# Moving the residuals, scalings and next transposes of the first four row blocks to later blocks in an output projection

## The chip, the cores and the metric

The kernel is one layer of a hybrid decoder, written for one core of a Trainium2 chip (trn2). The metric is device time in microseconds, the median of several runs. One execution of the kernel was also recorded by the hardware profiler; all rows quoted below come from that execution. Times in rows are microseconds from the start of its span, unless marked ns.

## The reference, cut to what matters

The input `x` has 1024 rows (tokens) of 1024 numbers, in float32.

```python
h = rmsnorm(x, mix_pre_norm)
proj = h @ w_in                               # attention and recurrence inputs
attn = rmsnorm(dilated_mixture_attention(...), attn_out_norm)
rec = hgrn2_recurrence(...)
mixed = concatenate([attn, rec], axis=-1) @ w_out          # output projection
x = x + rmsnorm(mixed, mix_post_norm)                      # residual
h = rmsnorm(x, mlp_pre_norm)                               # scaling
ff = square(relu(h @ w_ff1)) @ w_ff2
x = x + rmsnorm(ff, mlp_post_norm)
```

`rmsnorm` divides a row by the root of the mean of its squares (plus 1e-6) and multiplies by a gain. The change concerns the lines from `mixed` to the second `h`, and the transposes that prepare `h` for the product with `w_ff1`.

## The kernel before

The rows are handled in eight blocks `t` of 128 rows (`NT = 8`). Matrix products are made in three passes: each operand is split into a high part (copied by ScalarE, ACT, line 83) and a low part (the rest, subtracted by VectorE, DVE, line 84), and TensorE (PE) multiplies high by high, high by low and low by high (lines 87, 88, 89). The order of instructions on each engine is the order of the program text: nothing is reordered. Where an instruction needs a result of another engine, or a buffer that is still in use, its engine waits, and everything behind it on that engine waits too. DMAs are issued by the queue SP, also in program order.

The output projection is the loop `for t in range(NT)` at lines 1000 to 1028. Its steps, with the engines that they use:

- `late_out(t, hf)` (line 833): the matmuls of one half (512 columns) of block `t` into a PSUM bank `pwo`. The banks have the tag "mm" for even `t` and "s" for odd `t`, two banks of each; so block `t` takes the banks of block `t - 2`. For `t < NE = 4` the recurrent half of the product was made earlier and lies in SBUF as `esum`; only 4 of the 8 slices of 128 are left, that is 12 matmuls per half. From block 4 on a half has 24.
- `row_turn(t + 1, which)` (line 800): four transposes on PE (`pmt`, line 812), then the split into `mt` on ACT and DVE. It prepares the left operand of the next block. Blocks before 4 need one such call here, later ones two.
- `row_attn(t + 2)` (line 794): two DVE instructions that scale a row block (lines 796, 798). `row_norm(t + 3)` (line 777): its squares on ACT (`dm`, lines 783 and 784) and its scale on GpSimd (POOL). `row_rec(t + 3)` (line 770): a product on POOL. `row_load(t + 4)` (line 762): its DMA.
- `mixed_half(t, hf)` (line 847): for `t < 4` DVE adds the bank to `esum` (line 856), which frees the bank; then ACT squares and sums the half (`dp`, line 858). After the second half POOL makes the scale `prp` (lines 863, 79, 80). In the first half it also issues the reload of `x` for the next block (`x_again`, line 843), into a buffer `xres` of the tag "P", which has three.
- `residual(t)` (line 866): per half DVE multiplies by `prp` and the gain (line 876; for `t >= 4` it reads the PSUM bank and so frees it) and adds `x` (line 877); ACT squares and sums the result (`dx`, line 878). Then SP stores the block (`x2d`, line 879) and POOL makes the next scale `x2r`.
- `residual_b(t)` (line 883): one DVE instruction over the whole block, with `x2r` and the gain of the next norm (line 889). For `t < 4` it writes into `esum`, for `t = 4` in place, later into a slab `x2n`.
- `next_turn(t)` (line 891): for each of two halves `kh` four transposes on PE into a bank `ph` of the tag "t" (two banks, line 899), and a copy by ACT into `hraw` (line 905). `split_tokens` in iterations 4 and 6 splits two finished blocks of `hraw` into `h2` (ACT and DVE).

In iteration `t` the kernel before runs `residual(t - 1)` ahead of `mixed_half(t, 0)`, and, behind the second half's matmuls, `next_turn(t - 2)` and `residual_b(t - 1)`. After the loop follow the first matmuls with `w_ff1`, with `residual`, `residual_b` and `next_turn` of the last blocks between them.

Small columns (one number per row) come from a tag with four buffers, `c1`, by the helper `col`.

Of the kernel before, what the change touches and what calls it, by code (L numbers as in the profile page):

```python
# [8 lines left out]
F32 = mybir.dt.float32  # L9
# [8 lines left out]
P = 128  # L18
# [3 lines left out]
NT = T // P  # L22
# [13 lines left out]
def hymba_layer(ctx, tc, x, w_in, w_out, w_ff1, w_ff2, g_pre, lb_logits, g_mix, g_post,  # L36
# [9 lines left out]
    tp = ctx.enter_context(tc.tile_pool(name="tiny", bufs=4))  # L46
# [3 lines left out]
    def slab(tag, name, dtype=F32, shape=(P, T)):  # L50
        return sp.tile(list(shape), dtype, tag=tag, name=name,
                       bufs={"S": 9, "T": 9, "P": 3, "BT": 2, "V8": 2, "R": 1}[tag])

    def bank(tag, name):
        return ps.tile([P, 512], F32, tag=tag, name=name,
                       bufs={"mm": 2, "s": 2, "t": 2, "pv": 2}[tag])

    def half(name, dtype=F32):
        return sp.tile([P, 512], dtype, tag="half", name=name, bufs=2)

    def col(name, n=1):
        return tp.tile([P, n], F32, tag=f"c{n}", name=name)
# [14 lines left out]
    def rsqrt_mean(dst, ssum, n, width):  # L77
        t = col("ms", width)
        G.tensor_scalar(t, ssum, 1.0 / n, EPS, op0=ALU.mult, op1=ALU.add)  # L79
        G.tensor_tensor(out=dst, in0=t, in1=nhalf[:, :width], op=ALU.pow)  # L80
# [653 lines left out]
    rows, xress, mts, pmo, gains, scales = {}, {}, {}, {}, {}, {}  # L734
    AL = (AH // 2 - 1) * P

    def load_gain(name, tag, src):
        gains[name] = slab(tag, name)
        nc.sync.dma_start(out=gains[name], in_=src.partition_broadcast(P))
# [19 lines left out]
    def early_sum(t):  # L759
        return early["sum"][t // 2][:, t % 2]  # L760

    def row_load(t):
        row = rows[t] = slab("S", f"row{t}")
        c = AW if t < NE else 0
        nc.sync.dma_start(out=row[:, c:AW + AL], in_=mix_dram[t * P:(t + 1) * P, c:AW + AL])
# [11 lines left out]
    def row_norm(t):  # L777
        row = rows[t]
        dump = half(f"dm{t}")
        ss = col("ass", 2)  # L780
        sa = col("asa")
        ra = scales["row", t] = tp.tile([P, 1], F32, tag="era", name=f"era{t}") if t < NE else col("ara")
        S.activation(dump[:, :AL], row[:, AW:AW + AL], AF.Square, accum_out=ss[:, 0:1])
        S.activation(dump[:, AL:AW], row_fin(t), AF.Square, accum_out=ss[:, 1:2])
        G.tensor_tensor(out=sa, in0=ss[:, 0:1], in1=ss[:, 1:2], op=ALU.add)
        rsqrt_mean(ra, sa, AW, 1)

    def row_gain(t):

        row, gmix = rows[t], gains["gmix"]  # L790
        G.tensor_tensor(out=row[:, AW:AW + AL], in0=row[:, AW:AW + AL], in1=gmix[:, AW:AW + AL], op=ALU.mult)
        G.tensor_tensor(out=row[:, AW + AL:], in0=row_fin(t), in1=gmix[:, AW + AL:], op=ALU.mult)

    def row_attn(t):
        row, gmix, ra = rows[t], gains["gmix"], scales.pop(("row", t))
        V.scalar_tensor_tensor(row[:, AW:AW + AL], row[:, AW:AW + AL], ra, gmix[:, AW:AW + AL],
                               op0=ALU.mult, op1=ALU.mult)
        V.scalar_tensor_tensor(row[:, AW + AL:], row_fin(t), ra, gmix[:, AW + AL:], op0=ALU.mult, op1=ALU.mult)

    def row_turn(t, which, late=False):  # L800

        if t < NE and which == 0:
            dst = early["mt"][t // 2][:, t % 2]
        else:
            if (t, 1) not in mts and (t, 0) not in mts or t < NE:
                mts[t] = slab("V8", f"mt{t}", F32R, (P, 2, 2, 4, P))
            dst = mts[t][:, which]
        mts[t, which] = dst
        src = rec_row(t) if which == 0 else rows[t][:, AW:]
        pt = bank("pv" if late else "t", f"pmt{t}_{which}")  # L810
        for j in range(4):
            TE.transpose(pt[:, j * P:(j + 1) * P], src[:, j * P:(j + 1) * P], ident)
        split_into(dst[:, 0], dst[:, 1], pt.rearrange("p (j c) -> p j c", j=4))
# [19 lines left out]
    def late_out(t, hf):  # L833
        pm = pmo[t, hf] = bank("s" if t % 2 else "mm", f"pwo{t}_{hf}")
        if t >= NE:
            run(out_mm(t, hf, 0, pm, True, False))
        run(out_mm(t, hf, 1, pm, t < NE, True))
# [5 lines left out]
    def x_again(t):  # L843
        xress[t] = slab("P", f"xres{t}")
        nc.sync.dma_start(out=xress[t], in_=x[t * P:(t + 1) * P, :])

    def mixed_half(t, hf):

        if hf == 0:
            if t + 1 < NT:  # L850
                x_again(t + 1)
            scales["mix", t] = col("pss", 2)
        src = pmo[t, hf]
        if t < NE:
            whole = early_sum(t)[:, hf * 512:hf * 512 + 512]
            V.scalar_tensor_tensor(whole, src, scales["row", t], whole, op0=ALU.mult, op1=ALU.add)
            src = pmo[t, hf] = whole
        S.activation(half(f"dp{t}{hf}"), src, AF.Square, accum_out=scales["mix", t][:, hf:hf + 1])
        if hf == 1:
            s2 = scales.pop(("mix", t))  # L860
            s1 = col("ps1")
            rp = scales["mix", t] = col("prp")
            G.tensor_tensor(out=s1, in0=s2[:, 0:1], in1=s2[:, 1:2], op=ALU.add)
            rsqrt_mean(rp, s1, D, 1)

    def residual(t):
        xr = xress[t]
        rp = scales.pop(("mix", t))
        s4 = col("x2h", 2)
        s3 = col("x2s")  # L870
        r3 = scales["x2", t] = col("x2r")
        for hf in range(2):
            sl = slice(hf * 512, hf * 512 + 512)
            src = pmo.pop((t, hf))
            add = src if t < NE else half(f"ad{t}{hf}")
            V.scalar_tensor_tensor(add, src, rp, gains["gpost"][:, sl], op0=ALU.mult, op1=ALU.mult)
            V.tensor_tensor(out=xr[:, sl], in0=add, in1=xr[:, sl], op=ALU.add)
            S.activation(half(f"dx{t}{hf}"), xr[:, sl], AF.Square, accum_out=s4[:, hf:hf + 1])
        nc.sync.dma_start(out=x2_dram[t], in_=xr)
        G.tensor_tensor(out=s3, in0=s4[:, 0:1], in1=s4[:, 1:2], op=ALU.add)  # L880
        rsqrt_mean(r3, s3, D, 1)

    def residual_b(t):
        xr = xress[t]
        if t < NE:
            xress[t] = early_sum(t)
        elif t >= NT - 3:
            xress[t] = slab("S", f"x2n{t}")
        V.scalar_tensor_tensor(xress[t], xr, scales.pop(("x2", t)), gains["gmlp"], op0=ALU.mult, op1=ALU.mult)

    def next_turn(t):

        xr = xress.pop(t)
        th, c = t // 4, (t % 4) * P
        for kh in range(2):
            pt = bank("t", f"ph2{t}_{kh}")
            for j in range(4):
                k = kh * 4 + j
                TE.transpose(pt[:, j * P:(j + 1) * P], xr[:, k * P:(k + 1) * P], ident)
            src = pt.rearrange("p (j c) -> p j c", j=4)  # L900
            if t % 4 == 0:
                hraw[kh, th] = wide.tile([P, 4, 512], F32, tag="A", name=f"hraw{kh}{th}")
                if th == 0:
                    h2[kh] = tuple(wide.tile([P, 4, 512], F32R, tag="A", name=f"h2{q}{kh}") for q in "hl")
            S.activation(hraw[kh, th][:, :, c:c + P], src, AF.Copy)
# [91 lines left out]
    load_gain("gpost", "T", g_post)  # L997
    load_gain("gmlp", "T", g_mlp)
    h2, hraw = {}, {}
    for t in range(NT):  # L1000
        late_out(t, 0)
        if t > 0 and t + 1 < NT:
            for which in range(t + 1 < NE, 2):
                row_turn(t + 1, which, True)
            if t + 4 < NT:
                row_load(t + 4)
        if NE <= t + 2 < NT:
            row_attn(t + 2)
        if t > 0:
            residual(t - 1)  # L1010
        mixed_half(t, 0)
        late_out(t, 1)
        if t > 1:
            next_turn(t - 2)
        if t > 0:
            residual_b(t - 1)
        if t + 3 < NT:
            row_norm(t + 3)
            if t + 3 < NE:
                row_gain(t + 3)  # L1020
        if t in (4, 6):
            for kh in range(2):
                split_tokens(kh, (t - 4) * P)
        if t == 4:
            w_get(W10, 0)
        mixed_half(t, 1)
        if NE <= t + 3 < NT:
            row_rec(t + 3)

# [584 lines left out]
    x2r, plain, praw = {}, {}, {}  # L1614
# [105 lines left out]
    t, pieces, rf = late  # L1720
# [71 lines left out]
```

## Time and profile before

| | us |
|---|---|
| median of 3 runs | 1289.68 |
| lowest and highest run | 1286.98, 1290.79 |
| profiled execution | 1289.73 |
| its span | 1287.9 |

Over the span PE is busy for 97%, DVE for 69%, ACT for 41% and POOL for 23%. The loop of the output projection runs from about 571 to 652 us.

A row of the timeline gives the start, the duration, the engine, the line, the operation with its output and inputs, the shape and the count; in brackets stands how long the engine was idle before it, and which engine, tile and line ended that. Matmuls overlap: a matmul of 512 columns lasts about 0.39 us, but the next starts after 0.23. So work on PE is measured here from start to start. A row of the windows gives the stretch, its length, the busy time of PE, PE's weight loads, DVE, ACT and POOL (with counts), the granted clock of PE as a share of full speed, the busy share of the DMA engines, and GB/s.

### The profile page before, as it was taken

The numbers are of one execution on the slowest core, as the hardware profiler recorded it, in microseconds if no ns is written. First come the engines' busy times: TensorE is split into PE (matmuls) and PEld (weight loads), VectorE is DVE, ScalarE is ACT, GpSimd is POOL, SyncE is SP. The second block draws the span as 40 slices with busy tenths as digits, with TensorE's granted clock in tenths as the row PEclk, the third lists the DMA queues.
The fourth block names the chain that finished last, engine by engine and source line by source line (L and its number), as shares of the span: only waits on it lengthen the run. The fifth ranks groups of instructions, "written<-read, shape, count | busy, mean of one in ns | idle before, by whom it ended". The sixth has DMA issues, their size and how long they took to land. (4 is left out here: it accounts for less than half of the span.)

```text
span 1287.9 us, 17288 instructions
## 1 busy us (share of the span) xinstructions
PE 1247.8 (97%) x6524; PEld 1061.3 (82%) x6524; DVE 885.1 (69%) x1524; ACT 533.3 (41%) x967; POOL 297.8 (23%) x308
## 2 busy tenths in 40 slices
PE   8999999999999998999999899999999999999997
PEld 8898989888888887887877788888878888888886
DVE  5686868675666666667658766666676776688956
ACT  6623232213555556564555322222235533344412
POOL 0000000012122223043250487575541000000012
PEclk9999999999999999898999999999999999999999
DMA  5201111123222323335242344443369454434423
GB/s 205 67 17 50 34 50 33 34 82 88 61 83 66 83 66 110 98 114 179 94 152 90 139 173 177 148 180 131 139 245 353 161 196 131 160 102 131 155 76 129
DMA packets 58578, 153.98 MB, mean 120 GB/s; under 512 B 4992, under 2 KB 12928, under 8 KB 58240
## 3 DMA queue, kind: packets, MB, share of 16 engines
q1 hardware_dynamic: 58496, 152.89, 35.1%
q8 instruction: 51, 0.84, 0.3%
q14 instruction: 31, 0.25, 0.1%
HBM read 106.73 MB, written 39.85 MB: 114 GB/s over the span
## 5 line engine op out<-in xcount | busy, mean ns | idle before, releaser
L87 PE MATMUL f<-bh,ah 128*128 128x512 f32 x392 | 152.5, 389 | 0.0
L88 PE MATMUL f<-bl,ah 128*128 128x512 f32 x392 | 152.5, 389 | 0.0
L89 PE MATMUL f<-bh,al 128*128 128x512 f32 x392 | 152.5, 389 | 0.0
L84 DVE TENSOR_TENSOR al<-ar,ah 128x1024 fp32r<-128x1024 f32 x49 | 60.6, 1236 | 48.2 <-ACT ah L83 17.6
L87 PEld LDWEIGHTS f<-bh,ah 128*128 128x128 f32 x392 | 73.6, 188 | 15.4
L89 PEld LDWEIGHTS f<-bh,al 128*128 128x128 f32 x392 | 73.6, 188 | 15.3
L88 PEld LDWEIGHTS f<-bl,ah 128*128 128x128 f32 x392 | 73.6, 188 | 15.1
L83 ACT ACTIVATE ah<-ar 128x1024 fp32r<-128x1024 f32 x49 | 52.0, 1062 | 48.8 <-DMA ar<-actd 22.0
L1707 POOL TENSOR_SCALAR fp<-fss 128x1 f32<-128x1 f32 x8 | 3.5, 432 | 267.4 <-ACT fd L1704 267.4
L670 DVE CUSTOM_DVE_ANT_0 p<-ps,bt 128x512 f32<-128x512 f32 (+2 forms) x84 | 44.3, 552 | 25.0 <-PE ps L668 24.8
L697 ACT ACTIVATE pth<-pt 128x512 fp32r<-128x512 f32 (+2 forms) x96 | 43.3, 486 | 42.3 <-PE pt L694 40.6
L698 DVE TENSOR_TENSOR ptl<-pt,pth 128x512 fp32r<-128x512 f32 (+2 forms) x96 | 50.2, 551 | 15.3 <-ACT pth L697 15.2
L681 ACT ACTIVATE p<-p,nm 128x128 f32<-128x128 f32 (+3 forms) x64 | 49.5, 773 | 9.3 <-DVE nm L676 6.2
L727 POOL TENSOR_TENSOR anat<-anat,rd 128x128 f32<-128x128 f32 x32 | 14.6, 455 | 150.5 <-DVE anat L726 146.9
L79 POOL TENSOR_SCALAR ms<-hss 128x8 f32<-128x8 f32 x4 | 0.8, 197 | 206.3 <-DVE hss L538 206.3
L83 ACT ACTIVATE bh<-br 128x1024 fp32r<-128x1024 f32 x28 | 29.7, 1060 | 43.2 <-PE f L89 37.9
L694 PE MATMUL pt<-ident,p 128*128 128x128 f32 x288 | 42.9, 276 | 4.7 <-DVE ptl L698 4.7
L1221 POOL TENSOR_TENSOR e<-x,e 128x512 f32<-128x512 f32 x14 | 20.6, 1473 | 102.5 <-DVE x L1172 102.5
L84 DVE TENSOR_TENSOR wl<-raw,wh 128x1024 fp32r<-128x1024 f32 x23 | 31.4, 1365 | 18.3 <-ACT wh L83 18.0
L694 PEld LDWEIGHTS pt<-ident,p 128*128 128x128 f32 x288 | 33.5, 141 | 9.3 <-DVE ptl L698 6.8
L711 PE MATMUL pov<-pth,v 128*128 128x256 f32 (+1 forms) x160 | 40.6, 288 | 0.0
L1574 DVE TENSOR_TENSOR acc<-f,acc 128x512 f32<-128x512 f32 x52 | 33.8, 684 | 8.3 <-PE f L89 8.3
(1615 smaller groups left out, 3905.9 us busy)
## 6 DMA issues: line engine op xcount, KB each, us to landing
ar<-actd SPq DMA_DIRECT2D x49, 512.0 KB, 3.7
raw<-in_w_in_dram SPq DMA_DIRECT2D x28, 512.0 KB, 3.6
w1r<-in_w_ff_dram SPq DMA_DIRECT2D x14, 1024.0 KB, 6.6
br<-in_w_ff_dram SPq DMA_DIRECT2D x14, 1024.0 KB, 7.2
actd<-e SPq DMA_DIRECT2D x17, 768.0 KB, 4.1
actd<-e SPq DMA_DIRECT2D x11, 1024.0 KB, 4.0
xr<-in_x_dram SPq DMA_DIRECT2D x8, 512.0 KB, 9.5
raw<-in_w_out_dram SPq DMA_DIRECT2D x8, 512.0 KB, 3.6
```

Source lines behind the costliest of these rows:

```text
L83: S.activation(hi, src, AF.Copy)
L84: eng.tensor_tensor(out=lo, in0=src, in1=f32(hi), op=ALU.subtract)
L87: TE.matmul(dst, lhs[0], rhs[0], start=start, stop=False)
L88: TE.matmul(dst, lhs[0], rhs[1], start=False, stop=False)
L89: TE.matmul(dst, lhs[1], rhs[0], start=False, stop=stop)
L670: V.tensor_tensor_reduce(out=pe[:, k0:k0 + n], in0=pS[:, :n], in1=bts[hd][:, o:o + n], scale=1.0, scalar=-3.0e38, op0=ALU.add, op1=ALU.max ...
L681: S.activation(pe[:, :nk], pe[:, :nk], AF.Exp, bias=nm[:, b:b + 1], accum_out=dn[:, b:b + 1])
L694: TE.transpose(pt[:, j * P:(j + 1) * P], pe[:, jj * P:(jj + 1) * P], ident)
L697: S.activation(hi, src, AF.Copy)
L698: V.tensor_tensor(out=lo, in0=src, in1=f32(hi), op=ALU.subtract)
L711: TE.matmul(po[:, c0:256], vst, pt[j // 4][q][:, j % 4, c0:], start=j == 0 and q == 0, stop=j == nj - 1 and q == 1)
L1574: V.tensor_tensor(out=acc_at(p, i), in0=pm, in1=acc_at(p, i), op=ALU.add)
```

## The change

Residuals, scalings and next transposes of blocks are issued at other places of the loop, given by three tables: `RES` (residual, ahead of `mixed_half(t, 0)`), `RES_B` (residual_b, ahead of RES), `TURN` (next_turn, behind the second half's matmuls). Residual 0 and 1 stand at the end of iterations 1 and 2. The places, before and after:

| block | residual, before | after | residual_b, before | after | next_turn, before | after |
|---|---|---|---|---|---|---|
| 0 | 1 | end of 1 | 1 | 2 | 2 | 3 |
| 1 | 2 | end of 2 | 2 | 3 | 3 | 4 |
| 2 | 3 | 4 | 3 | 5 | 4 | 5 |
| 3 | 4 | 5 | 4 | 6 | 5 | 6 |
| 4 | 5 | 5 | 5 | 6 | 6 | 6 |
| 5 | 6 | 6 | 6 | 7 | 7 | 7 |
| 6 | 7 | 7 | 7 | 7 | after the loop | after the loop |

Block 7 follows after the loop in both. The reload of `x` for block `r + 3` now follows residual_b of block `r`, whose buffer it takes. Two of the small columns, `prp` and `x2r`, get tags of their own with two buffers each.

```diff
     def mixed_half(t, hf):
         if hf == 0:
-            if t + 1 < NT:
-                x_again(t + 1)
             scales["mix", t] = col("pss", 2)
...
-            rp = scales["mix", t] = col("prp")
+            rp = scales["mix", t] = tp.tile([P, 1], F32, tag="prp", name=f"prp{t}", bufs=2)
...
     def residual(t):
-        r3 = scales["x2", t] = col("x2r")
+        r3 = scales["x2", t] = tp.tile([P, 1], F32, tag="x2r", name=f"x2r{t}", bufs=2)
...
+    RES = {4: (2,), 5: (3, 4), 6: (5,), 7: (6,)}
+    RES_B = {2: (0,), 3: (1,), 5: (2,), 6: (3, 4), 7: (5,)}
+    TURN = {3: (0,), 4: (1,), 5: (2,), 6: (3, 4), 7: (5,)}
     for t in range(NT):
         late_out(t, 0)
...
         if NE <= t + 2 < NT:
             row_attn(t + 2)
-        if t > 0:
-            residual(t - 1)
+        for r in RES_B.get(t, ()):
+            residual_b(r)
+        if t < 2:
+            x_again(t + 1)
+        for r in RES.get(t, ()):
+            residual(r)
         mixed_half(t, 0)
         late_out(t, 1)
-        if t > 1:
-            next_turn(t - 2)
-        if t > 0:
+        for r in TURN.get(t, ()):
+            next_turn(r)
+        for r in RES_B.get(t, ()):
+            if r + 3 < NT:
+                x_again(r + 3)
+        if t == NT - 1:
             residual_b(t - 1)
         if t + 3 < NT:
             row_norm(t + 3)
...
         mixed_half(t, 1)
+        if t in (1, 2):
+            residual(t - 1)
         if NE <= t + 3 < NT:
             row_rec(t + 3)
```

## The prediction

> **What bounds the kernel now.** I read the page first, then the granted clock by windows around the changed stage (571 to 652 us), then the timeline of each engine there. On the page TensorE (PE) is busy nearly all the time, and one slice of the changed stage shows a lowered clock.
>
> ```profile
> span 1287.9 us, 17288 instructions
> PE 1247.8 (97%) x6524; PEld 1061.3 (82%) x6524; DVE 885.1 (69%) x1524; ACT 533.3 (41%) x967; POOL 297.8 (23%) x308
> PEclk9999999999999999898999999999999999999999
> ```
>
> ```profile
> 596.00:598.00 2.00, 0.44 (x2) 0.02 (x1) 1.07 (x1) 2.00 (x8) 0.74 (x2) 1.00 1.00 295
> 602.00:604.00 2.00, 2.00 (x6) 1.51 (x6) 1.97 (x4) 0.00 (x0) 0.11 (x1) 0.50 0.00 0
> ```
>
> The second fence shows windows (length, then PE busy; the granted clock is the third number from the end). PE nearly stands still in one, and some microseconds later it is busy throughout at half clock. The timeline of PE names the place.
>
> ```profile
> 576.76 0.39 PE L87 MATMUL pwo<-woh,mt 128*128 128x512 f32 x1
> 579.49 0.60 PE L812 MATMUL pmt<-ident,row 128*128 128x128 f32 x4
> 582.47 0.39 PE L89 MATMUL pwo<-woh,mt 128*128 128x512 f32 x1
> 588.64 1.03 PE L899 MATMUL ph<-ident,esum 128*128 128x128 f32 x8
> 589.54 0.50 PE L87 MATMUL pwo<-woh,mt 128*128 128x512 f32 x1
> 592.67 1.03 PE L812 MATMUL pmt<-ident,row 128*128 128x128 f32 x8
> 596.05 0.39 PE L89 MATMUL pwo<-woh,mt 128*128 128x512 f32 x1
> 598.36 1.06 PE L899 MATMUL ph<-ident,esum 128*128 128x128 f32 x8 [1.92 <-DVE esum L889]
> 600.22 0.79 PE L87 MATMUL pwo<-wh,mt 128*128 128x512 f32 x1 [0.80 <-ACT mt L83]
> 608.63 1.03 PE L812 MATMUL pmt<-ident,row 128*128 128x128 f32 x8
> 615.76 0.48 PE L87 MATMUL pwo<-wh,mt 128*128 128x512 f32 x1
> 621.30 1.03 PE L812 MATMUL pmt<-ident,row 128*128 128x128 f32 x8
> 628.42 0.48 PE L87 MATMUL pwo<-wh,mt 128*128 128x512 f32 x1
> ```
>
> A half block of twelve matmuls takes 2.73 us (576.76 to 579.49); of 24 matmuls, 5.54 (615.76 to 621.30). At 598.36 the transposes of block 1 wait 1.92 us for its scaling (L889), and at 600.22 block 4 waits 0.80 for its split on ACT. The 24 matmuls that follow take 8.41 us (600.22 to 608.63), 2.87 too many, at half clock. Block 3's first half takes 3.13 instead of 2.73 (589.54 to 592.67), 0.40 too many. So the stage loses 1.92 + 0.80 + 2.87 + 0.40 = 6.0 us, and this is all that the change can win. The reason: blocks 0 to 3 have only half of PE's work left (twelve matmuls per half), but all of DVE's and ACT's.
>
> **What the change moves.** No instruction goes or comes; residual and residual_b of blocks 0 to 3 and next_turn of blocks 0 to 4 shift between iterations. Every engine keeps to program order, so I lay the new order along the rows. First the durations that I need.
>
> ```profile
> 580.75 0.69 DVE L84 TENSOR_TENSOR mt<-pmt,mt 128x512 fp32r<-128x512 f32 x1 [3.04 <-ACT mt L83]
> 588.91 0.58 ACT L83 ACTIVATE mt<-pmt 128x512 fp32r<-128x512 f32 x1
> 590.13 1.73 DVE L796 SCALAR_TENSOR_TENSOR row<-row,ara,gmix 128x384 f32<-128x384 f32 x1
> 592.04 0.74 DVE L876 SCALAR_TENSOR_TENSOR esum<-esum,prp,gpost 128x512 f32<-128x512 f32 x1
> 594.81 0.74 DVE L856 SCALAR_TENSOR_TENSOR esum<-pwo,era,esum 128x512 f32<-128x512 f32 x1
> 594.99 0.63 ACT L878 ACTIVATE dx<-xres 128x512 f32<-128x512 f32 x1 [0.59 <-DVE xres L877]
> 595.52 0.19 ACT L878 ACTIVATION_READ_ACCUMULATOR dx<-xres 128x1 f32 x1
> 596.93 1.28 DVE L889 SCALAR_TENSOR_TENSOR esum<-xres,x2r,gmlp 128x1024 f32<-128x1024 f32 x1 [1.37 <-POOL x2r L80]
> 598.13 0.74 DVE L856 SCALAR_TENSOR_TENSOR esum<-pwo,era,esum 128x512 f32<-128x512 f32 x1
> 610.88 1.29 DVE L84 TENSOR_TENSOR mt<-pmt,mt 128x512 fp32r<-128x512 f32 x2 [1.34 <-ACT mt L83]
> 626.72 0.74 DVE L876 SCALAR_TENSOR_TENSOR ad<-pwo,prp,gpost 128x512 f32<-128x512 f32 x1
> ```
>
> Residual costs DVE 2.77 us (592.04 to 594.81), residual_b 1.20 (596.93 to 598.13), row_attn 1.91 (590.13 to 592.04), an addition of mixed_half 0.7; the squares of a residual cost ACT 0.72 (594.99 to the end of the readout, 595.71).
>
> *First place, block 4's first matmul.* Residual(0) now stands behind block 1's second addition: pwo ends at 582.86, the addition takes DVE to 583.6, residual(0) to 586.4. ACT's squares end at 587.2, block 3's split on ACT (0.58) at 587.8 and on DVE at 588.4, just before PE wants it (588.64); the 0.40 goes. DVE then does row_attn(4) to 590.3, residual_b(0) to 591.5, two additions to 592.9, residual(1) to 595.6. ACT squares it until 596.4 and only then splits block 4, at 597.0. PE comes there, without next_turn(0) at 588.64, by 2.73 + 0.8 + 2.8 + 0.9 at 595.85. It waits 1.15, and its third matmul some 0.25 more for the low part. The old wait of 1.92 is gone, because next_turn(0) comes long after residual_b(0); what is late next is the split of block 4, behind the squares of block 1. New loss: 1.4.
>
> *Second place, block 6's first matmul.* It writes the PSUM bank of block 4, which residual(4) frees with its first L876. From the split of block 5 on DVE (610.88) to that instruction (626.72) were 15.84 us; the new iteration 5 puts residual_b(2) and residual(3) in front of it, 1.20 + 2.77, which makes 19.81. That the old residual_b(3) no longer stands on this path wins nothing, since the next item (the split of h2) waited for ACT anyway. PE's own way from block 5's transposes (608.63) to block 6 (628.42) is 19.79 and stays. So the wait is DVE's lag behind the transposes at block 5, plus 0.75 for the instruction and 0.05. The lag was 2.25 (608.63 to 610.88); the smallest in this stage was 1.26 (579.49 to 580.75). I take 2.25, because copies and squares still stand ahead of this split on ACT. The loss is 3.05, at least 2.05. Some 0.4 of it shows at next_turn(2), which waits for residual_b(2).
>
> *Third place, next_turn(4).* Iteration 6 issues next_turn(3) and next_turn(4) back to back; each takes two PSUM banks of the tag "t", which has two. So block 4's transposes wait until ACT has copied block 3's first bank.
>
> ```profile
> 639.51 0.63 ACT L878 ACTIVATE dx<-xres 128x512 f32<-128x512 f32 x1 [0.71 <-DVE xres L877]
> 640.14 0.58 ACT L858 ACTIVATE dp<-pwo 128x512 f32<-128x512 f32 x1
> 640.30 1.03 PE L899 MATMUL ph<-ident,xres 128*128 128x128 f32 x8
> 640.93 1.09 ACT L905 ACTIVATE hraw<-ph 128x512 f32<-128x512 f32 x2
> 641.09 0.48 PE L87 MATMUL pwo<-wh,mt 128*128 128x512 f32 x1
> 641.40 0.33 SPq L845 DMA_DIRECT2D xres<-in_x_dram  x1
> ```
>
> ```profile
> DMA to landing us min/median/max: 2.8/3.8/9.6
> ```
>
> Before, ACT was ready for this copy just when PE had transposed. Now residual_b(3) and residual_b(4) stand between block 7's split and residual(5) on DVE, 2 x 1.20, and all of dx, dp, hraw comes 2.40 later: dx 641.91, dp 642.55, copy 643.2 to 643.75. PE is ready at 641.1, on this clock, and goes on at 643.85: 2.75 lost. DVE can't start earlier, since block 7's split, which needs PE, stands ahead. The second next_turn itself (0.8) costs nothing new, it only comes later.
>
> *DMAs.* The reloads of x move on SP: x(6) now stands behind the store of block 5, at about 642, and lands at 646 by the median of 3.8; residual(6) uses it in the next iteration, some 8 us after the issue. The worst landing, 9.6, would cost DVE 2 us that PE doesn't wait for. x(7) still waits for next_turn(4) to free its buffer (641.40). The row loads keep their lead. The two small columns with buffers of their own add no instruction. All this is hidden.
>
> **Sum.** Old losses 6.0, new ones 1.4 + 3.05 + 2.75 = 7.2: 1.2 us longer before any clock effect. Now the clock. Besides the old stall, three waits of PE elsewhere bear on it or on what follows the stage:
>
> ```profile
> 333.64 0.50 PE L667 MATMUL ps<-kh,q 128*128 128x512 f32 x1 [1.18 <-DVE mx L670]
> 656.63 0.51 PE L1155 MATMUL f11a<-h2h,wl 128*128 128x512 f32 x1 [0.34 <-DVE wl L84]
> 715.88 0.80 PE L1155 MATMUL f12d<-T10h,ws 128*128 128x512 f32 x1 [2.55 <-DVE ws L84]
> 719.21 0.40 PE L1154 MATMUL f12d<-T11l,ws 128*128 128x512 f32 x1
> ```
>
> After the wait of 2.55, eight matmuls take 3.33 us instead of 1.85: 1.5 lost. After the old gap (596.44 to 600.22, 3.8 without a matmul, transposes inside) 2.87 was lost. The gap at block 6 has the same form (0.4 of wait, transposes, 2.6 of wait: 3.8); I take 2.2, between the two. The third has 2.75 unbroken: 1.5 by its nearest row. The first, 1.15, is left at nothing, by the wait of 1.18 at 333.64, behind which the first matmul took 0.50 and not 0.80 as at 715.88; its bound above is 1.5.
>
> [...]
>
> The profiled execution took 1289.73 (span 1287.9 and 1.8 around it), 0.05 above the median of the runs. After the stage PE and the splits hang on its last matmuls (PE's next wait is 0.34, at 656.63, for a split), so a shift goes through; the wait of 2.55 above is the most that could take some of it in, and it hangs on DVE's chain, which shifts too. Forecast: 1289.7 + 1.2 + 2.2 + 1.5 = **1294.6**.
>
> **Rivals.**
> *The clock stays up.* The two new waits come, but no half clock, or only one short stretch. For it: the wait of 1.18 cost no clock, and the new ones are each shorter than the old gap. Against it: 2.55 at 715.88. Time: 1290.9, with one stretch 1292.4; within 0.3%. [...]
> *Faster.* DVE, relieved in iterations 1 to 3, is ahead by iteration 5, and residual(4) frees its bank before PE asks. It decides at 2.25 + 0.8 = 3.05 us: DVE must reach block 5's split that much earlier against the transposes. Then the second gap and its clock go; if ACT also leads by 2.75 at next_turn(4), only the 1.4 is left: 1289.7 - 6.0 + 1.4 = 1285.1. Against it: the lag can't fall below 1.26, as the split follows the transposes.
> *The old stall does not go,* because the squares of residual(1) on ACT hold block 4's split by more than 1.15 and the clock falls there too: about 1.5 on top, 1296 to 1298.
>
> **Chances.** Forecast 0.50; clock stays up 0.37; faster 0.09; old stall too 0.04. A difference under 0.3% (3.9 us) counts as none; the forecast, +4.9, is just beyond. So slower 0.54, same 0.37, faster 0.09. Range: below, both waits with the smaller lag and no slow stretch, 1289.7 + 1.2 - 1.0 = 1289.9, less 2 for the spread of the runs; above, both stretches at 2.87 and 1.0 more at the first place, 1297.6. That is 1288 to 1298.
>
> **What would show it.** Right: no wait for L889 at next_turn(1); about 1.2 of wait for ACT's mt at block 4; PE waiting 2 to 3 us for DVE's L876 (ad) at block 6's first L87 and for ACT's hraw at the transposes of block 4; a granted clock of 0.5 for 3 to 6 us behind one or both. Wrong: no wait on L876 or hraw, or a full clock behind them.

## The result and the profile after

| | before | after |
|---|---|---|
| median of 8 runs, us | 1290.51 | 1294.39 |
| lowest and highest, us | 1286.98, 1291.62 | 1291.97, 1296.11 |
| profiled execution, us | 1289.73 | 1294.30 |
| its span, us | 1287.9 | 1292.5 |

The ratio is 1.0038, with a 95% interval of 1.0028 to 1.0048: slower by 0.38%, some 5 us. (The ratio isn't worked out from the medians; these are 3.9 us apart.)

The first view lists whom PE waited for in the kernel after, in the stretch 565 to 660 us (engine, tile and line; who was waited for; us in total, times, longest).

```profile
PE ph L897 <- ACT hraw L903: 2.4, 1, 2.4
PE pwo L87 <- DVE ad L874: 2.3, 1, 2.3
PE ph L897 <- DVE esum L887: 1.5, 1, 1.5
PE pwo L87 <- ACT mt L83: 0.9, 1, 0.9
```

The old wait of 1.92 for L889 at next_turn(1) is gone. The wait at block 4 for its split on ACT, 0.80 before, is still there with 0.88, and three others are new. All four lie in the three places of the prediction. (Behind the diff, L874, L887, L897 and L903 are the old L876, L889, L899 and L905.) The timeline of PE and, for the instructions that it waits for, of DVE and ACT, after:

```profile
570.43 0.60 PE L812 MATMUL pmt<-ident,row 128*128 128x128 f32 x4
594.55 1.03 PE L897 MATMUL ph<-ident,esum 128*128 128x128 f32 x8
596.47 0.50 PE L87 MATMUL pwo<-wh,mt 128*128 128x512 f32 x1 [0.88 <-ACT mt L83]
602.32 1.03 PE L812 MATMUL pmt<-ident,row 128*128 128x128 f32 x8
622.99 1.06 PE L897 MATMUL ph<-ident,esum 128*128 128x128 f32 x8 [1.52 <-DVE esum L887]
626.34 0.78 PE L87 MATMUL pwo<-wh,mt 128*128 128x512 f32 x1 [2.28 <-DVE ad L874]
633.52 1.03 PE L812 MATMUL pmt<-ident,row 128*128 128x128 f32 x8
639.86 1.03 PE L897 MATMUL ph<-ident,esum 128*128 128x128 f32 x8
643.29 1.86 PE L897 MATMUL ph<-ident,xres 128*128 128x128 f32 x8 [2.40 <-ACT hraw L903]
644.81 0.78 PE L87 MATMUL pwo<-wh,mt 128*128 128x512 f32 x1
656.78 1.03 PE L897 MATMUL ph<-ident,x2n 128*128 128x128 f32 x8
```

```profile
605.20 1.29 DVE L84 TENSOR_TENSOR mt<-pmt,mt 128x512 fp32r<-128x512 f32 x2 [3.07 <-ACT mt L83]
625.54 0.74 DVE L874 SCALAR_TENSOR_TENSOR ad<-pwo,prp,gpost 128x512 f32<-128x512 f32 x1
635.99 1.28 DVE L887 SCALAR_TENSOR_TENSOR esum<-xres,x2r,gmlp 128x1024 f32<-128x1024 f32 x1
637.19 1.28 DVE L887 SCALAR_TENSOR_TENSOR xres<-xres,x2r,gmlp 128x1024 f32<-128x1024 f32 x1
642.65 1.07 ACT L903 ACTIVATE hraw<-ph 128x512 f32<-128x512 f32 x2
```

The granted clock of PE, third number from the end, in windows behind the second and the third place, after:

```profile
626.00:628.00 2.00, 1.67 (x4) 1.39 (x5) 1.90 (x4) 1.16 (x4) 1.29 (x3) 0.60 0.64 262
628.00:630.00 2.00, 2.00 (x6) 1.57 (x6) 0.52 (x1) 1.39 (x5) 0.42 (x3) 0.55 0.33 135
642.00:644.00 2.00, 0.71 (x4) 0.71 (x5) 0.00 (x0) 1.73 (x6) 0.93 (x3) 0.86 0.95 299
644.00:646.00 2.00, 2.00 (x9) 1.81 (x8) 0.00 (x0) 1.41 (x3) 0.00 (x0) 0.50 0.64 234
646.00:648.00 2.00, 2.00 (x9) 1.60 (x8) 1.24 (x2) 2.00 (x3) 0.00 (x0) 0.78 0.82 240
```

A measure of the stage alone is the way from the transposes of block 1 (570.43) to those of next_turn(5) (656.78): 86.35 us. In the kernel before it was 652.07 - 570.70 = 81.37. So the stage itself is 5.0 us longer, the span of these two executions 4.6: the loss arises here. This length is used for each experiment below, because single executions also differ elsewhere (see the end).

### The profile page after: what moved, and what is told of

It is laid out like the page before. It is cut to its first block, busy times and chain, and to the rows that moved or that the text cites. A ratio compares the mean times of both kernels' runs of the same rounds, so it can differ in the third digit from the quotient of the medians.

```text
span 1292.5 us, 17284 instructions
## 1 busy us (share of the span) xinstructions
PE 1248.4 (97%) x6524; PEld 1062.3 (82%) x6524; DVE 885.7 (69%) x1524; ACT 533.1 (41%) x967; POOL 300.0 (23%) x308
```

## The experiments

The theory under test: engines keep to program order, so the place of a step in DVE's and ACT's queue makes the waits, and the two larger waits lower PE's clock, which costs extra. An instance of that order in the kernel after: DVE is idle for 6.27 us ahead of block 7's split (634.79), and the two scalings behind it in the text start only at 635.99 and 637.19; in the first run below, where they stand ahead of that split, they start at 626.72 and 629.93. The rivals stand in the expectations. The first four ran against the kernel before at a median of 1289.52, the last two at 1289.46. Gains against the changed kernel are worked out from the ratios to the kernel before, with 0.1% as 1.29 us. Ratio and medians differ by up to 0.09%, some 1.2 us, so the stage stands beside them; it comes from one execution of each kernel.

| kernel | ratio to before, 95% interval | median, us | stage, us |
|---|---|---|---|
| changed | 1.0038 (1.0028 to 1.0048) | 1294.39 | 86.35 |
| scalings first | 1.0018 (1.0007 to 1.0030) | 1292.09 | 82.46 |
| residuals swapped | 1.0021 (1.0011 to 1.0031) | 1292.69 | 84.80 |
| changed, PE's waits filled | 1.0005 (0.9996 to 1.0013) | 1291.27 | 83.22 |
| both orders, residual_b(2) early | 0.9989 (0.9979 to 0.9999) | 1289.31 | 80.97 |
| steps in DVE's gaps | 0.9968 (0.9956 to 0.9979) | 1285.40 | 76.57 |
| before, PE's waits filled | 1.0001 (0.9992 to 1.0010) | 1289.13 | 80.55 |

**Scalings first (third place alone).**

```diff
         late_out(t, 0)
+        for r in RES_B[6] if t == 6 else ():
+            residual_b(r)
         if t > 0 and t + 1 < NT:
             for which in range(t + 1 < NE, 2):
...
-        for r in RES_B.get(t, ()):
+        for r in RES_B.get(t, ()) if t != 6 else ():
             residual_b(r)
```

> Changed kernel, but in iteration 6 residual_b(3) and residual_b(4) stand ahead of block 7's split (row_turn(7)) instead of behind it. In-order theory: DVE does them in the 6.3 us that it waits for that split, dx, dp and the copy of block 3 come 2.4 us earlier, and the wait of 2.40 at the transposes of block 4 goes, and with it the half clock behind it (1.7): 1294.4 - 2.2 - 1.7 = 1290.5. The waits at block 6 (1.52 and 2.28) stay. Rival (the third wait is that of two banks too few, whatever ACT does): the wait stays at 2 us or more, 1294.

The timeline of PE at the second and the third place, and of DVE ahead of the third:

```profile
624.61 0.79 PE L87 MATMUL pwo<-wh,mt 128*128 128x512 f32 x1 [2.29 <-DVE ad L874]
639.16 1.15 PE L897 MATMUL ph<-ident,xres 128*128 128x128 f32 x8 [0.25 <-ACT hraw L903]
...
629.93 1.28 DVE L887 SCALAR_TENSOR_TENSOR xres<-xres,x2r,gmlp 128x1024 f32<-128x1024 f32 x1 [1.94 <-DMA x2d<-xres]
```

The wait of 2.40 is down to 0.25 with the same two banks, so the wait hung on the order on DVE, and through it on when ACT came to the copy, as the theory has it; the rival falls. The stage is 3.9 us shorter, as expected. The median gains less, 2.6 us by the ratios, but its interval reaches up to the expected 3.9; whether something else takes a little back, the runs don't tell. Something new shows: residual_b(4) works in place, and DVE waits 1.94 us for the store of that buffer.

**Residuals swapped (second place alone).**

```diff
-    RES = {4: (2,), 5: (3, 4), 6: (5,), 7: (6,)}
+    RES = {4: (2,), 5: (4, 3), 6: (5,), 7: (6,)}
```

> Changed kernel, but iteration 5 issues residual(4) ahead of residual(3). In-order theory: the bank that block 6 wants is freed 2.8 us earlier, the wait of 2.28 for DVE at block 6 goes to 0 to 0.3, the half clock behind it (1.6) goes, the wait of 1.5 for residual_b(2) stays: 1294.4 - 2.2 - 1.6 = 1290.6. The third place keeps 2.4. Rival (DVE has too much work in this stretch, whatever its order): the wait moves to another instruction, 1293 to 1295.

```profile
621.23 1.06 PE L897 MATMUL ph<-ident,esum 128*128 128x128 f32 x8 [1.52 <-DVE esum L887]
638.73 1.97 PE L897 MATMUL ph<-ident,xres 128*128 128x128 f32 x8 [3.73 <-ACT hraw L903]
640.35 0.78 PE L87 MATMUL pwo<-wh,mt 128*128 128x512 f32 x1
```

```profile
627.64 1.03 PE L812 MATMUL pmt<-ident,row 128*128 128x128 f32 x8
629.58 1.11 ACT L83 ACTIVATE mt<-pmt 128x512 fp32r<-128x512 f32 x2
```

The wait at block 6's first matmul is gone, as the order says. But the third wait grew from 2.40 to 3.73, so 1.3 of the 2.3 came back, with a longer half clock (6.8 us instead of 3.4). The second fence gives the reason: block 7's transposes start at 627.64, but on ACT the squares of residual(3) and all that queues behind them come first, and the split starts at 629.58, 1.9 us later (0.6 in the changed kernel, 633.52 to 634.16). So the theory was right about the second place, and the rival was right that part of the wait moves: the two places aren't independent. The stage is 1.6 us shorter, not 3.8.

**PE's waits filled (the clock alone).**

```diff
+    def fill_pe(n, tag, mt):
+        pm = bank("pv", f"fill{tag}")
+        wh = parts[WO0 + 1][0]
+        for _ in range(n):
+            TE.matmul(pm, mt[:, 0, 0], wh[:, :512], start=True, stop=True)
...
+        if t == 6:
+            fill_pe(8, "b", mts[6, 0])
         late_out(t, 0)
...
         for r in TURN.get(t, ()):
+            if r == 2:
+                fill_pe(5, "a", mts[6, 0])
+            if r == 4:
+                fill_pe(9, "c", mts[6, 0])
             next_turn(r)
```

> Changed kernel, all orders and waits kept, but PE does matmuls of no use (into a bank nobody reads) in its waits: 5 ahead of next_turn(2), 8 ahead of block 6, 9 between next_turn(3) and next_turn(4); by 0.23 each they fit into the waits of 1.52, 2.28 and 2.40. Clock theory: the waits end at the same instants, but the clock stays at 1.0 behind them, and what the half clock cost (1.6 and 1.7) is won: 1291.1. Rival (the slow matmuls there are slow for another reason, such as data just written): half clock or slow rows remain, 1294 or, with the filling in the way, more.

The matmuls go into a bank that nobody reads. Timeline of PE, and the clock by windows:

```profile
621.14 1.09 PE L897 MATMUL ph<-ident,esum 128*128 128x128 f32 x8 [0.31 <-DVE esum L887]
621.99 2.11 PE L1002 MATMUL fillb<-woh,mt 128*128 128x512 f32 x8
624.58 0.50 PE L87 MATMUL pwo<-wh,mt 128*128 128x512 f32 x1 [0.48 <-DVE ad L874]
630.16 1.03 PE L812 MATMUL pmt<-ident,row 128*128 128x128 f32 x8
```

```profile
626.00:628.00 2.00, 2.00 (x10) 1.64 (x10) 0.72 (x2) 1.29 (x6) 0.47 (x3) 1.00 0.21 88
640.00:642.00 2.00, 2.00 (x13) 1.75 (x14) 0.00 (x0) 1.74 (x4) 0.00 (x1) 1.00 0.91 287
```

Block 6 starts when DVE lets it, 55.9 us behind the start of the stage as in the changed kernel, but now at full clock: its 24 matmuls take 5.58 us (624.58 to 630.16) instead of 7.18. The stage is 3.1 us shorter (expected 3.3), the ratio falls by 0.33%. PE did 22 matmuls more and the kernel became faster, so the rival is out. Without the price of the clock the changed kernel would be nearly level with the one before. That isn't like against like, though, since the kernel before has a slow stretch of its own: with the waits filled in both (see the last run), the stage is still 2.7 us longer with the change (83.22 against 80.55).

**Both orders, and residual_b(2) early.** The edits of the first two, and `residual_b(2)` with the reload behind it in iteration 4, ahead of the split of h2.

> Both orders of the first two runs, and residual_b(2) moved into iteration 4 ahead of the split of h2, where DVE waits 4.1 us for ACT. In-order theory: all three waits behind block 5 go (1.52, 2.28, 2.40) with both half clocks (1.6, 1.7); only the wait of 0.9 at block 4 is left: 1294.4 - 9.3 = 1285.1, some 5 us faster than before. Rival (DVE and ACT bound the stage, so that waits only move): no better than 1290.

The waits at block 6 are gone, but 2.51 of the third stays:

```profile
628.80 1.28 DVE L887 SCALAR_TENSOR_TENSOR esum<-xres,x2r,gmlp 128x1024 f32<-128x1024 f32 x1 [2.04 <-POOL x2r L80]
631.20 1.28 DVE L84 TENSOR_TENSOR mt<-pmt,mt 128x512 fp32r<-128x512 f32 x2
637.31 1.46 PE L897 MATMUL ph<-ident,xres 128*128 128x128 f32 x8 [2.51 <-ACT hraw L903]
```

Residual(3), now the later of the two, delivers its scale late; residual_b(3) waits 2.04 for it and holds block 7's split on DVE, which stands behind it (631.20). ACT comes late to its part of that split too, at 629.58, as in the run with the residuals swapped; what each of the two costs was not separated. The expected 1285 was missed by 4 us: the stage is 5.4 us shorter, not 9.3. By the ratio the kernel is just faster than the one before; the medians are 0.2 us apart.

**Steps in DVE's gaps.** Blocks 0 and 1 as changed; the rest where DVE was seen waiting.

```diff
-    RES = {4: (2,), 5: (3, 4), 6: (5,), 7: (6,)}
-    RES_B = {2: (0,), 3: (1,), 5: (2,), 6: (3, 4), 7: (5,)}
-    TURN = {3: (0,), 4: (1,), 5: (2,), 6: (3, 4), 7: (5,)}
+    RES = {4: (), 5: (4,), 6: (5,), 7: (6,)}
+    RES_B = {2: (0,), 3: (1,), 4: (2,), 7: (5,)}
+    TURN = {3: (0,), 4: (1,), 5: (2,), 6: (4,), 7: (5,)}
...
         late_out(t, 0)
+        if t == 6:
+            next_turn(3)
+            residual_b(4)
...
         for r in RES.get(t, ()):
             residual(r)
+        if t == 5:
+            residual_b(3)
         mixed_half(t, 0)
...
+        if t in (5, 6):
+            x_again(t + 1)
...
+        if t == 4:
+            residual(3)
         if t in (4, 6):
...
         mixed_half(t, 1)
-        if t in (1, 2):
+        if t in (1, 2, 3):
             residual(t - 1)
```

> Changed kernel for blocks 0 and 1; from block 2 on the steps are laid where DVE sat waiting: residual(2) at the end of iteration 3, residual_b(2) early and residual(3) late in iteration 4 (ahead of the split of h2), residual_b(3) behind residual(4) in iteration 5, next_turn(3) right behind the first half of block 6 and residual_b(4) ahead of block 7's split; next_turn(4) alone at its old place. In-order theory: residual(4) is the first residual of iteration 5 and frees its bank in time (wait at block 6 0 to 0.5), the copies of block 3 are made half a block before next_turn(4) needs the banks (wait 0 to 0.3); only the 0.9 at block 4 is left, no half clock in the stage: 1294.4 - 9 = 1285, 4.5 us faster than the kernel before. Rival (DVE and ACT bound the stage, waits only move): 1288 or more.

The reloads of x for blocks 6 and 7 are issued in iterations 5 and 6. PE's wait in the stage, and the second and the third place on its timeline:

```profile
PE pwo L87 <- ACT mt L83: 0.9, 1, 0.9
```

```profile
621.74 1.03 PE L897 MATMUL ph<-ident,esum 128*128 128x128 f32 x8
628.44 1.03 PE L897 MATMUL ph<-ident,esum 128*128 128x128 f32 x8
635.65 1.03 PE L897 MATMUL ph<-ident,xres 128*128 128x128 f32 x8
```

Only the wait at block 4 is left, no transposes wait, the clock stays at 1.00, and the stage is 9.8 us shorter than in the changed kernel and 4.8 shorter than before. The median of 1285.40 beats both kernels, by 0.32% the one before (interval 0.21% to 0.44%). The rival is out: DVE and ACT had enough time, the order was what was missing. No run moved the wait at block 4.

**Before, PE's waits filled.**

```diff
+        if t == 4:
+            fill_pe(3, "b", mts[3, 1])
         late_out(t, 0)
...
+        if t == 3:
+            fill_pe(7, "a", mts[3, 1])
         if t > 1:
             next_turn(t - 2)
```

The helper `fill_pe` is that of the other filling, but its bank is one of the tag "mm".

> Kernel before, its order kept, but PE fills its two waits with matmuls of no use: 7 ahead of next_turn(1), 3 ahead of block 4 (0.23 each, into waits of 1.92 and 0.80). Both theories: the clock stays at 1.0 behind 600 us, where 2.87 was lost. Theory A (DVE's backlog was hidden behind the slow clock): with PE 2.9 us earlier, residual(4) is late for block 6, a wait of 1.4 to 2.6 for DVE's L876 appears there, and little is won, 1288.5 to 1290. Theory B (the prediction's old losses of 6.0 were all there was to win): no new wait, 1289.5 - 2.9 = 1286.6.

```profile
597.71 1.06 PE L899 MATMUL ph<-ident,esum 128*128 128x128 f32 x8 [0.34 <-DVE esum L889]
605.42 1.04 PE L812 MATMUL pmt<-ident,row 128*128 128x128 f32 x8
626.07 0.74 DVE L876 SCALAR_TENSOR_TENSOR ad<-pwo,prp,gpost 128x512 f32<-128x512 f32 x1
626.95 0.47 PE L87 MATMUL pwo<-wh,mt 128*128 128x512 f32 x1 [1.49 <-DVE ad L876]
```

The slow matmuls behind 600 us are gone, but a wait of 1.49 for residual(4) appears at block 6, where the kernel before had none. DVE reaches that instruction 56.0 us behind the start of the stage in both kernels (626.07 - 570.08 here, 626.72 - 570.70 before): it gained nothing from a faster PE. The stage is 0.8 us shorter, not 2.9, and the time is unchanged. So theory A holds: the half clock of the kernel before had hidden that DVE comes too late for block 6.

## Why the prediction was right

The forecast was 1294.6; the measured median is 1294.39. The mechanism came as forecast: three places, the named engines waited for, and a half clock behind the two larger waits. That the number is hit to 0.2 us is partly luck. The forecast started from 1289.7, the median of the kernel before in 3 runs; over 8 runs it is 1290.51, 0.8 higher. And the terms missed in both directions.

The terms are compared here from start to start, as the prediction took its own. The number in brackets on a row is smaller than what the wait costs: it counts from the end of the last matmul, and without the wait the next one would have started some 0.2 us before that end (640.30 and 1.03 long, but the next starts at 641.09). Without a wait, transposes take 0.79 to the next matmul and 24 matmuls 5.54.

- *First place.* Forecast 1.15 of wait for block 4's split behind the squares of residual(1), and 0.25 for its low part, 1.4 in all. Measured 1.44: 7.77 (594.55 to 602.32) instead of 6.33, with the same releaser. No clock was lost there, as taken (1.00 from 594 to 602), so the rival of the old stall is out. That the squares are the cause is read off ACT's rows (the split starts at 595.84, right behind them); no run tested it.
- *Second place.* Forecast 3.05 in two parts, 0.4 at next_turn(2) and the rest at block 6 for L876. Measured 4.23 (602.32 to 626.34 is 24.02, instead of 19.79), in brackets 1.52 at next_turn(2) and 2.28 at block 6. The terms account for it: DVE's lag at block 5 was 2.88 (602.32 to 605.20), not the 2.25 taken, and its way to residual(4) 20.34 (605.20 to 625.54), not 19.81. The prediction had looked only for a smaller lag, down to 1.26; it grew, and the rival *Faster*, which needs a smaller one, is out.
- *Third place.* Forecast 2.75 for ACT's copy. Measured 2.64 (639.86 to 643.29 is 3.43, instead of 0.79), in brackets 2.40. The two scalings stand ahead of residual(5) as forecast, at 635.99 and 637.19. That they are the cause is shown by moving just them: 0.25 in brackets.
- *The clock.* Forecast 2.2 and 1.5. Measured 1.64 behind block 6 (7.18 instead of 5.54), and 1.72 at the third place: the transposes of block 4 start 1.52 us ahead of the next matmul instead of 0.79, and the 48 matmuls of block 7 take 11.97 (644.81 to 656.78) instead of 10.98 (641.09 to 652.07 before). Filling the waits won 3.1 of the stage: shown. The rival "the clock stays up" is out.
- *The sum.* The new losses are 1.44 + 4.23 + 2.64 of waiting and 3.36 of clock, 11.7; forecast 10.9. The old ones, measured in the same way, are 2.08 and 1.07 of waiting, 2.87 of clock and 0.4 around block 3, 6.4; the prediction had read the two waits off the brackets and came to 6.0. That makes 5.2 more, where 4.9 was forecast. The stage grew by 5.0; the rest of 0.2 lies at its start, which was that much slower in the kernel before (8.79 from 570.70 to 579.49, against 8.62 from 570.43 to 579.05). So the second place was 1.2 too small, and the clock 0.3 and the old losses 0.4 made part of that up.
- *The bound.* That 6.0 us "is all that the change can win" stands as a bound, if 6.4 is put for it: the best order here won 4.8 of the stage. But its terms can't be won one by one. Taking away the half clock alone won 0.8 of 2.87, because the next wait, at block 6, comes out.
- *DMAs.* The reload of x for block 6 was issued at 641.80, against 642 forecast, and PE waited for none in the stage.

No single wait in the stage of the kernel after was over 2.64, and the clock fell behind two places. From the last matmul ahead of the waits to the first behind them, with transposes in between, 4.9 us passed at the second place and 4.8 us at the third. The clock also fell behind the wait of 2.54 shown at the end, which has no transposes in it. How long a gap must be for the clock to fall is not shown by these runs.

## What to carry to other kernels

Where every engine runs in program order, as in the rows here, a step that is moved away from one wait stands in front of something else (the two scalings ahead of residual(5): 2.40 us of wait at next_turn(4)): lay the new order along the durations of the old rows, engine by engine, and look for the next thing in the queue, the PSUM bank that a late reader holds and the buffer count of a tag. Put moved steps where their engine was seen waiting, not where the text has room; that turned a loss of 0.38% into a gain of 0.32% here, with as many instructions on each engine. Where a half clock followed a wait of PE, it cost a further 1.64 and 1.72 us in the stage after and 2.87 before, and matmuls of no use put into the wait are a cheap test for that price (with them the clock stayed at 1.00 from 586 to 660 in both kernels). Before a stall is counted as a gain, look for the wait that it hides.

## What the runs showed of the hardware

Up to PE's last matmul, the slow stretches have only two lengths, 3.4 and 6.8 us: in the whole profiles of the kernels before and after, and in the windows at 510 to 530, 586 to 660 and 706 to 728 us of the six others. In the kernel before, the clock was low from 599.44 to 606.28 (worked out from the windows that hold its ends, clock 0.86 at 598 to 600 and 0.93 at 606 to 608, with 0.50 in the whole windows between): 6.8 us. In the kernel after it was low from 626.4 to 629.8 and from 643.44 to 646.88: 3.4 us each, and the two start 17.04 us apart, five times 3.41. Two more start in the same profile, at 517.16 and at 721.96: 109.24 us ahead of 626.4 and 78.52 behind 643.44, which is 32 and 23 times 3.41.

Waits of one length did not cost the same in each profile. The wait of 2.55 in the next stage, which the prediction priced, shows it. First the kernel after, then the kernel before with PE's waits filled:

```profile
720.54 0.50 PE L1165 MATMUL f12d<-T10h,ws 128*128 128x512 f32 x1 [2.54 <-DVE ws L84]
```

```profile
714.42 0.50 PE L1166 MATMUL f12d<-T10h,ws 128*128 128x512 f32 x1 [2.55 <-DVE ws L84]
```

In the kernel after, the first matmul behind it still ran at full clock (0.50, not 0.80), and the clock fell only 1.4 us later, at about 722. In the kernel of the second row the clock did not fall behind it (1.00 from 706 to 728), nor did it behind the same wait in the profile of the steps in DVE's gaps (712.68; 1.00 from 706 to 720); in the other six it fell within the wait or up to 1.4 us later. Ahead of the loop, where all eight kernels are the same, PE pauses for 2.14 us up to 516.29 in the kernel before and up to 516.16 in the kernel after, and 6.8 us of half clock go with it. Of the other six profiles three show that stretch there, and three (scalings first, residuals swapped, the changed kernel with PE's waits filled) a clock of 1.00 from 510 to 530.

So the price of the clock at one place, read from one execution, can be another in the next, and this is part of why the length of the stage told the experiments apart better than one time of the whole. Of the other runs only the mean clock is on record, and it agrees: of the 35 runs of the kernel before beside the first four experiments, the ten with a mean clock of 0.991 took 1290.0 to 1292.9 us, the five with 0.996 or 0.997 took 1288.0 to 1288.8.
